# Raw weights in one ring of four halves, in a hybrid decoder step on one core of Trainium2

## The chip, the core and the metric

The kernel runs on one NeuronCore of one Trainium2 chip. The time is the device time of one execution in microseconds (us), from the first to the last instruction with what the launch adds around it. The engines of the core are named as in the profile: PE (TensorE, matrix products; PEld are its weight loads), ACT (ScalarE), DVE (VectorE), POOL (GpSimd) and SP (SyncE, which here only issues DMAs). The engines run their own instruction streams, each in its own fixed order, and wait for each other by semaphores.

## What is computed

One step of a decoder block over 520 tokens (512 of a new sequence, 8 single tokens that continue older ones), model width 1024, all in float32:

```python
h = x
h = h + 0.5 * swiglu(rms_norm(h, ffn1_norm), w_gate1, w_up1, w_down1)   # FFN width 2816
h = h + mixer(rms_norm(h, mix_norm), ...)     # causal pooling heads beside SSD (Mamba-2) heads
h = h + 0.5 * swiglu(rms_norm(h, ffn2_norm), w_gate2, w_up2, w_down2)
y = rms_norm(h, final_norm)

def swiglu(x, wg, wu, wd):
    return (silu(x @ wg) * (x @ wu)) @ wd
```

The change lies in how weights come on chip. Nearly all of its effect is to be looked for in the two FFNs and in the projections of the mixer.

## The kernel before

**Float32 by three products.** A weight block of 128 x 1024 arrives as raw float32 and is cut in two parts. ACT casts it to a rounded format (the tile `whi`), DVE subtracts the cast from the raw value and keeps the rest (`wlo`). A product then is three matmuls (`mm3`, lines 133, 136 and 137): high by high, high by low, low by high. Activations are cut in the same way.

**FFN tiles.** The 2816 columns are 22 tiles `f` of 128. A tile needs a gate block and an up block of 512 KB each: the pair that `raw_pair` returns, with the gate block in half 0 and the up block in half 1. Most tiles run through `Ffn.product`, which forms a block product of gate, up and x by seven products in place of eight (the scheme of Strassen and Winograd). Each product is 12 matmuls: products 1 and 2 use `d1` (the two parts of the gate block), 5 and 7 use `e1`, 6 and 3 use `e2` (parts of sums of the blocks, tiles `shi` and `slo`), 4 uses the second half of the up block (the quarter, tiles `qhi` and `qlo`).

The order on PE in the first FFN is written out in `stream`: product 1 of tile t, product 4 of the tile before, then 5, 6, 3, 7, 2 of tile t. Product 1 writes bank A; right after it ACT copies A, the snapshot of line 466, to the bank BE (or to the tile `ac`), and product 5 then accumulates on it. Product 7's snapshot must be taken before product 4 accumulates on bank A. Line 514 on DVE reads A when a tile is closed (`close`), and frees the bank for the tile after the next.

In the first FFN the tiles 0 and 1 run as plain float32 products (`plain`), tiles 2 to 21 through `stream`. After tiles 8 and 16 come four Down tiles each, `Down(c, d)`, which put the first 16 columns of blocks through the down projection in the same seven-product scheme (in the profile: `Down(c=0, d=0)` and so on). The last part of the down projection, and all of it in the second FFN, goes by units of one block (`load_unit`, line 129).

**What a tile does with its raw pair** (`load`, `sums`, `quarter`), for the first FFN from tile 4 on:

- SP issues two DMAs at line 367, half 0 and then half 1.
- ACT casts half 0 to `whi` (line 373) and writes its negative to `wlo` (line 374); a DMA that POOL issues adds the raw block to it in flight from HBM (line 375, an accumulating DMA). For a plain tile only the second 512 columns of `wlo` go this way, and DVE subtracts the first 512 (line 377); for a Down tile all 1024 go through ACT and the DMA (`n2` is 0).
- DVE forms the sums s1 (line 403, from both halves), and s2 in two steps (lines 404 and 405, from s1 and half 0). ACT and DVE cut s1 and s2 in parts (lines 121 and 123).
- The second half of half 1 is cut in `quarter`: ACT casts it (line 218 or 223) and DVE subtracts (line 224), or, for tiles up to 6, ACT and an accumulating DMA do it (lines 219 and 220).

So the last reader of half 0 is the second step of s2 at line 405, and that of half 1 is the quarter's low part at line 224 (for tiles up to 6 its cast).

**Raw buffers before.** `raw_pair` takes a new tile of two halves from the pool `wp`, with the tag `raw` and two buffers. A buffer is free for a new pair once every reader of both halves of the old pair is done. Units (`raw_tile`) take the halves of a pair one after the other, in the mixer too. The homes of `whi` and `wlo` are two buffers in the first FFN (`homes`, set ahead of `ffn1`), so tile t + 2 casts into the home of tile t once PE has run product 2 of tile t.

**The order of each engine.** The program is written as one stream. The framework (`TileContext(nc, schedule_with_timeline_sim=True)`) then lays down each engine's order ahead of time: a model of the timeline lets each engine take, among the instructions that are ready, the one of highest priority, which is by default the one written first. SP's DMAs are ordered in this way too. `tc.issue_after(i)`, inside `queued(...)`, puts the instructions of its block behind `i` on the engine of `i`. `tc.high_priority()` and `tc.keep_in_program_order()` do what they say. On the chip the order is fixed: an instruction whose data are late holds all that stand behind it on its engine.

**The second FFN** runs tile 0 as a plain product, woven into the end of the mixer (`LAST_PLAN`), and tiles 1 to 21 through `step`. The pair of tile 0 (`2_0`) is read by PE itself until the end of that weave.

Of the kernel before, what the change touches and what calls it, by code (L numbers as in the profile page):

```python
# [10 lines left out]
F32 = mybir.dt.float32  # L11
# [6 lines left out]
P = 128  # L18
# [45 lines left out]
def tile_trunk_step(ctx: ExitStack, tc: tile.TileContext, ins: dict, outs: dict):  # L64
    nc = tc.nc
# [6 lines left out]
    wp = ctx.enter_context(tc.tile_pool(name="wp", bufs=3, side="right"))  # L72
# [19 lines left out]
    def queued(*ins):  # L92
        stack = ExitStack()
        for i in ins:
            stack.enter_context(tc.issue_after(i))
        return stack

    def raw_pair(name):
        return wp.tile([P, 2, 1024], F32, tag="raw", bufs=2, name=f"raw_{name}")

    half, ends, added = [], [], []

    def raw_tile(name):
        if not half:
            t = raw_pair(name)
            half.extend([t[:, 1], t[:, 0]])
        return half.pop()
# [3 lines left out]
    def weight_homes(n, name, hp, nb, tags):  # L111
        if hp is wp:
            hp, nb, tags = homes.pop(0) if len(homes) > 1 else homes[0]
        return tuple(hp.tile([P, 1024], F32R, tag=t, bufs=nb, name=f"{t}_{name}")[:, :n] for t in tags)

    def split(src, n, name, hp, nb, tags, then=()):
        hi, lo = weight_homes(n, name, hp, nb, tags)
        h, l = hi, lo
        if len(src.shape) == 3:
            h, l = (t.rearrange("p (j c) -> p j c", j=src.shape[1]) for t in (hi, lo))  # L120
        cast = nc.scalar.copy(h, src)  # L121
        with queued(*then):
            low = nc.vector.tensor_tensor(out=l, in0=src, in1=h.bitcast(F32), op=ALU.subtract)
        ends[:] = cast.ins, low.ins
        return hi, lo
# [6 lines left out]
    def mm3(ps, whi, wlo, xhi, xlo, start, stop, pin=False, **kw):  # L132
        first = nc.tensor.matmul(ps, whi, xhi, start=start, stop=False, **kw)  # L133
        if pin:
            tc.keep_in_program_order(first)
        nc.tensor.matmul(ps, whi, xlo, start=False, stop=False, **kw)  # L136
        nc.tensor.matmul(ps, wlo, xhi, start=False, stop=stop, **kw)  # L137

    def ws(w, k, m=P):
        return w[:, k * m : (k + 1) * m]  # L140
# [102 lines left out]
    class Ffn:  # L243
# [15 lines left out]
        def plain_load(self, f, j=None, us=(0, 1), queue=nc.sync):  # L259
            if f not in self.raw:  # L260
                self.raw[f] = raw_pair(f"{self.i}_{f}")
            src = ins[f"w{self.i}gu"]
            for u in us:
                if j is None:
                    nc.sync.dma_start(out=self.raw[f][:, u], in_=src[2 * f + u])
                    continue
                q = (t.rearrange("p (q c) -> p q c", q=2)[:, :, j * P : j * P + P]
                     for t in (self.raw[f][:, u], src[2 * f + u]))
                queue.dma_start(out=next(q), in_=next(q))
# [86 lines left out]
        def load(self, f, first, then, by_dma):  # L356
            i, wx, src = self.i, self.wx, ins[f"w{self.i}gu"]
            n = f"{i}_{f}"
            raw = raw_pair(n)
            if isinstance(f, int):  # L360
                drams = [src[2 * f + u] for u in range(2)]
            else:
                lo = f.c * CHUNKS[0]
                drams = [ins[f"w{i}d"][2 * f.d + u, :, lo * P : (lo + 8) * P] for u in range(2)]
            self.dram[f] = drams
            for u in range(2):
                nc.sync.dma_start(out=raw[:, u], in_=drams[u])
            with queued(*first):
                if self.folded and (f, 0) not in LOW_ON_DVE:
                    d1 = weight_homes(1024, f"{n}a", wp, 3, ("whi", "wlo"))  # L370
                    hi, lo = d1
                    n2 = 512 if isinstance(f, int) else 0
                    nc.scalar.copy(hi, raw[:, 0])
                    nc.scalar.activation(out=lo[:, n2:], in_=hi[:, n2:].bitcast(F32), func=AF.Copy, scale=-1.0)
                    nc.gpsimd.dma_start(out=lo[:, n2:], in_=drams[0][:, n2:], accum_op=ALU.add)
                    if n2:
                        nc.vector.tensor_tensor(out=lo[:, :n2], in0=raw[:, 0, :n2], in1=hi[:, :n2].bitcast(F32), op=ALU.subtract)
                else:
                    d1 = split(raw[:, 0], 1024, f"{n}a", wp, 3, ("whi", "wlo"))
            with queued(*then, *(ends if by_dma and i == 1 else ())):  # L380
                self.sums(f, n, src, raw, d1, by_dma)
# [56 lines left out]
        def product(self, f, p):  # L438
            js = range(KD // 2)
            if f not in self.A:  # L440
                self.load(f, *self.behind.get(f, ((), (), False)))
                n = f"{self.i}_{f}"
                self.A[f] = ps[0].tile([P, 512], F32, tag="A", bufs=2, name=f"A{n}")
                self.BE[f] = ps[0].tile([P, 2, 512], F32, tag="BE", bufs=2, name=f"BE{n}")
                self.ac[f] = [self.wx.tile([P, 2, HB], F32, tag="ac", bufs=3, name=f"ac{n}_{q}") for q in range(2)]
            if p != 1 and 4 not in self.w[f]:
                self.quarter(f, self.held[f])
            slot, dst, opens = {1: (0, 0, True), 2: (1, 1, True), 5: (3, 2, True), 6: (5, 0, False),
                                3: (2, 2, False), 7: (4, 0, False), 4: (6, 0, False)}[p]
            opens = opens and (p != 2 or self.i == 2 or f in self.whole)  # L450
            out = self.A[f] if dst == 0 else self.BE[f][:, dst - 1]
            (whi, wlo), k = self.w[f][p]
            xth, xtl = self.nx[:2]
            for j in js:
                if isinstance(f, int):
                    x = xth[:, j, slot], xtl[:, j, slot]
                else:
                    x = (self.gs[f.c * CHUNKS[0] // 2 + j][:, q, {5: 6, 6: 5}.get(slot, slot)] for q in range(2))
                mm3(out[:, :HB], ws(whi, k[j]), ws(wlo, k[j]), *x, opens and j == 0,
                    j == KD // 2 - 1, pin=j == 0 and ((f, p) in ((2, 7), (3, 1)) or self.i == 1), skip_group_check=True)  # L460
            a, c = self.ac[f]
            if p == 1 and self.i == 1 and f not in self.whole:
                a = self.BE[f][:, :, :HB]
            keep = {1: a[:, 0], 6: a[:, 1], 7: c[:, 0], 5: c[:, 1]}.get(p)
            if keep is not None:
                self.copied = nc.scalar.copy(keep, out[:, :HB]).ins  # L466
            if p == 7:
                nc.vector.tensor_tensor(out=c[:, 0], in0=c[:, 0], in1=c[:, 1], op=ALU.add)

# [950 lines left out]
```

## Time and profile before

| | us |
|---|---|
| median of 3 runs | 978.33 |
| lowest and highest of them | 976.18 and 979.62 |
| the profiled execution | 978.69 |
| its span, first to last instruction | 976.9 |

The span and what lies around it (978.69 - 976.9 = 1.8 us) make up the time of the profiled execution. All times in the profile count from the start of the span. A row of the timeline gives start, duration, engine, line, operation and tiles (written <- read), and in brackets the idle time of the engine ahead of it with what ended it. A row of the waits gives who waited for whom: us in total, times, the longest. `PE A L137` is the instruction of PE at line 137 that writes tile A. A row of the stretches gives the stretch, its length, then for PE, PEld, DVE, ACT and POOL the busy us with the number of instructions, then the granted clock of PE, the share of the DMA engines and GB/s. A matmul of 260 columns has a duration of 0.28 us in the records, but matmuls overlap: where PE does not wait, they start 0.12 us apart, so waits of PE are read from the starts and from the number of matmuls in a stretch, not from its busy time alone.

### The profile page before, as it was taken

The numbers are of one execution on the slowest core, as the hardware profiler recorded it, in microseconds if no ns is written. First come the engines' busy times: TensorE is split into PE (matmuls) and PEld (weight loads), VectorE is DVE, ScalarE is ACT, GpSimd is POOL, SyncE is SP. The second block draws the span as 40 slices with busy tenths as digits, with TensorE's granted clock in tenths as the row PEclk, the third lists the DMA queues.
The fourth block names the chain that finished last, engine by engine and source line by source line (L and its number), as shares of the span: only waits on it lengthen the run. The fifth ranks groups of instructions, "written<-read, shape, count | busy, mean of one in ns | idle before, by whom it ended". The sixth has DMA issues, their size and how long they took to land.

```text
span 976.9 us, 19565 instructions
## 1 busy us (share of the span) xinstructions
PE 962.3 (99%) x7772; PEld 942.0 (96%) x7772; DVE 825.3 (84%) x1372; ACT 592.2 (61%) x1098; POOL 113.5 (12%) x192
## 2 busy tenths in 40 slices
PE   9999999999999999999999999999999999999996
PEld 8999999999999999999999999999999999999995
DVE  6899879998798688789978897999957999667886
ACT  7777656677566455485767565666643666515563
POOL 0111100001000000065331000100012000110010
PEclk9999999999999999999999999999999999999998
DMA  7565554445553343262443333433445433452232
GB/s 211 164 164 135 146 152 124 129 142 135 136 151 99 100 130 120 91 210 78 138 138 133 108 104 108 148 104 113 130 134 189 132 109 108 125 183 81 81 118 89
DMA packets 48444, 126.80 MB, mean 130 GB/s; under 512 B 7064, under 2 KB 15192, under 8 KB 48352
## 3 DMA queue, kind: packets, MB, share of 16 engines
q1 hardware_dynamic: 39840, 104.18, 31.7%
q0 software_dynamic: 8240, 21.24, 10.9%
q8 instruction: 61, 1.00, 0.4%
q14 instruction: 31, 0.25, 0.1%
q10 hardware_dynamic: 272, 0.13, 0.0%
HBM read 118.18 MB, written 7.34 MB: 128 GB/s over the span
## 4 chain that ended last, share of the span: by engine, by line
PE 68%; DVE 3%; DMA 1%; issue 1%; ACT 0%; DVEq 0%; SPq 0%; ACTq 0%
PE A L137 5%; PE A L133 5%; PE A L136 5%; PE dn L137 4%; PE dn L133 4%; PE dn L136 4%; PE BE L137 4%; PE BE L136 4%; PE BE L133 4%; PE wo L133 2%; PE wo L137 2%; PE wo L136 2%; PE inx L133 2%; PE inz L133 2%; PE inz L136 2%; PE inz L137 2%
## 5 line engine op out<-in xcount | busy, mean ns | idle before, releaser
L137 PE MATMUL dn<-g,wlo_2d 128*128 128x260 f32 x256 | 72.4, 283 | 0.0
L133 PE MATMUL dn<-g,whi_2d 128*128 128x260 f32 x256 | 72.1, 282 | 0.0
L136 PE MATMUL dn<-g,whi_2d 128*128 128x260 f32 x256 | 72.1, 282 | 0.0
L466 ACT COPY ac<-A 128x260 f32<-128x260 f32 x104 | 38.5, 372 | 31.1 <-PE A L137 29.4
L403 DVE TENSOR_TENSOR s<-raw 128x1024 f32<-128x1024 f32 x39 | 47.6, 1220 | 7.9 <-DMA raw<-in_w1gu 5.8
L133 PEld LDWEIGHTS dn<-g,whi_2d 128*128 128x128 f32 x256 | 48.2, 188 | 0.0
L136 PEld LDWEIGHTS dn<-g,whi_2d 128*128 128x128 f32 x256 | 48.2, 188 | 0.0
L137 PEld LDWEIGHTS dn<-g,wlo_2d 128*128 128x128 f32 x256 | 48.1, 188 | 0.0
L609 DVE SCALAR_TENSOR_TENSOR td<-dn,r_f 128x520 f32<-128x520 f32 (+1 forms) x25 | 16.8, 677 | 32.7 <-PE dn L137 32.7
L121 ACT CAST whi_2d<-raw_2d 128x1024 fp32r<-128x1024 f32 (+1 forms) x18 | 18.5, 1026 | 36.7 <-PE dn L136 15.0
L1148 POOL DMA_DIRECT2D out_nss<-hs x16 | 8.7, 545 | 259.3 <-DVE hs L1146 259.2
L133 PE MATMUL wo<-catg,whi_wo 128*128 128x260 f32 x128 | 37.1, 290 | 0.0
L133 PE MATMUL inz<-xh_mx,whi_inz 128*128 128x260 f32 x128 | 36.6, 286 | 0.0
L133 PE MATMUL inx<-xh_mx,whi_inx 128*128 128x260 f32 x128 | 36.4, 284 | 0.0
L137 PE MATMUL wo<-catg,wlo_wo 128*128 128x260 f32 x128 | 36.3, 283 | 0.0
L136 PE MATMUL inz<-xl_mx,whi_inz 128*128 128x260 f32 x128 | 36.2, 283 | 0.0
L137 PE MATMUL inz<-xh_mx,wlo_inz 128*128 128x260 f32 x128 | 36.2, 283 | 0.0
L136 PE MATMUL inx<-xl_mx,whi_inx 128*128 128x260 f32 x128 | 36.1, 282 | 0.0
L137 PE MATMUL inx<-xh_mx,wlo_inx 128*128 128x260 f32 x128 | 36.1, 282 | 0.0
L136 PE MATMUL wo<-catg,whi_wo 128*128 128x260 f32 x128 | 36.1, 282 | 0.0
L466 ACT COPY ac<-BE 128x260 f32<-128x260 f32 x41 | 15.4, 375 | 26.9 <-PE BE L137 18.5
L995 DVE SCALAR_TENSOR_TENSOR A<-U,h,A 128x544 f32<-128x544 f32 x36 | 28.9, 802 | 2.2 <-ACT A L993 1.8
(2154 smaller groups left out, 4377.8 us busy)
## 6 DMA issues: line engine op xcount, KB each, us to landing
raw<-in_w2gu SPq DMA_DIRECT2D x44, 512.0 KB, 4.4
raw<-in_w1gu SPq DMA_DIRECT2D x41, 512.0 KB, 4.5
raw_2d<-in_w2d SPq DMA_DIRECT2D x16, 512.0 KB, 4.5
raw_wo<-in_w_out SPq DMA_DIRECT2D x12, 512.0 KB, 4.3
ab<-scr_acs SPq DMA_DIRECT2D x8, 512.0 KB, 3.6
h<-in_state_ssm SPq DMA_DIRECT2D x16, 256.0 KB, 3.2
raw_inz<-in_w_in SPq DMA_DIRECT2D x8, 512.0 KB, 4.5
hs<-in_state_ssm POOLq DMA_DIRECT2D x16, 256.0 KB, 3.6
```

The source lines that it names most:

```text
L121: cast = nc.scalar.copy(h, src)
L133: first = nc.tensor.matmul(ps, whi, xhi, start=start, stop=False, **kw)
L136: nc.tensor.matmul(ps, whi, xlo, start=False, stop=False, **kw)
L137: nc.tensor.matmul(ps, wlo, xhi, start=False, stop=stop, **kw)
L403: nc.vector.tensor_tensor(out=s1, in0=diag, in1=up0, op=ALU.add)
L466: self.copied = nc.scalar.copy(keep, out[:, :HB]).ins
L609: nc.vector.scalar_tensor_tensor(out=o, in0=s, scalar=-0.5, in1=q, op0=ALU.mult, op1=ALU.mult)
L995: nc.vector.scalar_tensor_tensor(out=A[:, :n], in0=U[:, j : j + n], scalar=w(j), in1=A[:, :n], op0=ALU.mult, op1=ALU.add)
L1148: tc.keep_in_program_order(nc.gpsimd.dma_start(out=outs["nss"][:, b, 4 * g : 4 * g + 4], in_=hs))
```

## The change

All raw weights get one tile for the whole kernel, of two pairs of two halves, in place of a new tile per pair from two buffers. `raw_pair` counts its calls and returns the two pairs in turn; the framework then follows readers and writers by the part of the tile that they touch, so the DMA of a half waits for the readers of that half alone. One name, `2_2` (tile 2 of the second FFN), does not count: it gets the pair of the call before it, that of tile 1.

Two more edits come with it. In the first FFN the cast of tile 4's gate block, with the negated copy and the accumulating DMA that depend on it, is put behind the snapshot of product 7 of tile 2 on ACT. And for Down tiles with d = 3 (two of the eight), `n2` becomes 512: the first 512 columns of the low part are subtracted on DVE (line 377), and ACT's negated copy and the accumulating DMA carry only the other 512.

```diff
+    raws = wp.tile([P, 2, 2, 1024], F32, tag="raw", bufs=1, name="raw")
+    turns = []
+
     def raw_pair(name):
-        return wp.tile([P, 2, 1024], F32, tag="raw", bufs=2, name=f"raw_{name}")
+        if name != "2_2":
+            turns.append(name)
+        return raws[:, len(turns) % 2]
...
                 if self.folded and (f, 0) not in LOW_ON_DVE:
                     d1 = weight_homes(1024, f"{n}a", wp, 3, ("whi", "wlo"))
                     hi, lo = d1
-                    n2 = 512 if isinstance(f, int) else 0
-                    nc.scalar.copy(hi, raw[:, 0])
+                    n2 = 512 if isinstance(f, int) or f.d == 3 else 0
+                    with queued(*((self.tail,) if f == 4 else ())):
+                        nc.scalar.copy(hi, raw[:, 0])
...
             if keep is not None:
                 self.copied = nc.scalar.copy(keep, out[:, :HB]).ins
+                if (f, p) == (2, 7):
+                    self.tail = self.copied
```

## The prediction

> **What bounds the kernel now.** I read the page first, for the span and the engines:
>
> ```profile
> span 976.9 us, 19565 instructions
> PE 962.3 (99%) x7772; PEld 942.0 (96%) x7772; DVE 825.3 (84%) x1372; ACT 592.2 (61%) x1098; POOL 113.5 (12%) x192
> ```
>
> TensorE (PE) sets the time: it is busy in 962.3 of 976.9 us, and every other engine has room on the average. So a change can win only what PE waits, and can lose anything that makes it wait more. Where it waits I took from the table by stretches; its number in brackets after PE busy counts the matmuls.
>
> ```profile
> 54.00:114.00 60.00, 59.90 (x497) 59.52 (x496) 56.34 (x89) 45.61 (x74) 7.56 (x9) 1.00 0.57 141
> 114.00:167.00 53.00, 51.90 (x425) 51.06 (x424) 45.69 (x72) 30.73 (x49) 4.19 (x5) 1.00 0.54 148
> 167.00:229.00 62.00, 61.78 (x510) 61.18 (x509) 58.23 (x92) 43.63 (x72) 5.03 (x6) 1.00 0.49 134
> 229.00:292.00 63.00, 61.44 (x508) 60.83 (x507) 52.49 (x82) 37.81 (x60) 5.04 (x6) 1.00 0.53 139
> 292.00:355.00 63.00, 63.00 (x528) 63.00 (x528) 48.90 (x93) 34.35 (x65) 2.10 (x3) 1.00 0.34 102
> 653.00:714.00 61.00, 61.00 (x510) 61.00 (x509) 55.16 (x77) 39.44 (x67) 0.00 (x0) 1.00 0.32 104
> ```
>
> The clock column is 1.00 throughout. In the last two stretches PE never waits and does 528/63.00 = 8.38 and 510/61.00 = 8.36 matmuls per us, one per 0.12 us. At 8.37 the second stretch should hold 444 matmuls and has 425, a loss of 19 x 0.12 = 2.2 us; the fourth should hold 527 and has 508, also 2.2 us; the first lacks 5 (0.6 us), the third 9 (1.1 us). All four lie in the first FFN's streamed tiles. The second FFN (last row) loses nothing. What ends those waits is in the view of waits of the weight loads:
>
> ```profile
> PEld BE L133 <- ACT BE L466: 2.2, 4, 0.9
> PEld BE_Down(c=1, d=2)_2976 L133 <- ACT BE_Down(c=1, d=2)_2976 L466: 1.2, 1, 1.2
> PEld A L133 <- ACT ac L466: 0.9, 2, 0.7
> PEld A L133 <- DVE gq L514: 0.8, 3, 0.3
> PEld BE L137 <- DVE slo_2c L123: 0.5, 1, 0.5
> PEld BE_Down(c=0, d=2)_1441 L133 <- ACT BE_Down(c=0, d=2)_1441 L466: 0.4, 1, 0.4
> PEld A L137 <- DMA qlo_6b<-in_w1gu: 0.3, 1, 0.3
> ```
>
> Four of the seven rows name ScalarE's (ACT) snapshot at line 466, which copies the finished product 1 out of bank A so that product 5 may accumulate on it: 2.2 + 1.2 + 0.4 = 3.8 us in six tiles, and one more of 0.7 us at the start. Why the snapshot is late, the timeline of ACT and PE at one of the six shows:
>
> ```profile
> 272.10 1.05 ACT L373 CAST whi_18a<-raw 128x1024 fp32r<-128x1024 f32 x1 [1.50 <-DMA raw<-in_w1gu]
> 273.18 0.64 ACT L374 ACTIVATE wlo_18a<-whi_18a 128x512 fp32r<-128x512 f32 x1
> 273.72 0.37 ACT L466 COPY BE<-A 128x260 f32<-128x260 f32 x1
> 270.51 0.28 PE L137 MATMUL BE_Down(c=1, d=3)_3100<-gs,wlo_Down(c=1, d=3)a 128*128 128x260 f32 x1
> 273.38 0.28 PE L137 MATMUL A_Down(c=1, d=3)_3099<-gs,qlo_Down(c=1, d=3)b 128*128 128x260 f32 x1
> 274.14 0.39 PE L133 MATMUL BE<-xth_f,shi_17c 128*128 128x260 f32 x1 [0.48 <-ACT BE L466]
> ```
>
> ACT idles 1.50 us for the raw weights of the next tile, 18, then casts them, makes their negated copy, and only then takes tile 17's snapshot, which stands behind them in its order. PE, due at 273.50, starts at 274.14: 0.64 us late, and its first matmul takes 0.39 instead of 0.28 us. The cast could have run from 270.79, when PE ended its last use of the weight home that the cast overwrites (270.51 + 0.28). A tile whose weights had landed in time shows that this order alone does no harm:
>
> ```profile
> 177.64 1.05 ACT L373 CAST whi_13a<-raw 128x1024 fp32r<-128x1024 f32 x1
> 178.73 0.63 ACT L374 ACTIVATE wlo_13a<-whi_13a 128x512 fp32r<-128x512 f32 x1
> 179.53 0.36 ACT L466 COPY BE<-A 128x260 f32<-128x260 f32 x1 [0.17 <-PE A L137]
> ```
>
> Here the snapshot waited for PE, not PE for it. So in six tiles PE pays for a late load.
>
> **The change part by part.** *The ring.* Before, a pair of halves (gate weights, up weights) is one buffer, and both halves load when the last reader of the pair is done. Tile 17's pair, which frees tile 19's:
>
> ```profile
> 267.63 0.68 DVE L224 TENSOR_TENSOR qlo_Down(c=1, d=3)b<-raw_Down(c=1, d=3)_3074,qhi_Down(c=1, d=3)b 128x512 fp32r<-128x512 f32 x1
> 268.23 0.69 DVE L405 TENSOR_TENSOR s<-s,raw 128x512 f32<-128x512 f32 x1
> 277.27 0.68 DVE L224 TENSOR_TENSOR qlo_17b<-raw,qhi_17b 128x512 fp32r<-128x512 f32 x1
> 282.54 1.05 ACT L373 CAST whi_19a<-raw 128x1024 fp32r<-128x1024 f32 x1 [1.14 <-DMA raw<-in_w1gu]
> 283.84 1.22 DVE L403 TENSOR_TENSOR s<-raw 128x1024 f32<-128x1024 f32 x1 [0.76 <-DMA raw<-in_w1gu]
> ```
>
> The gate half's last reader is the sum at line 405, done at 268.92; the up half's is the quarter's low part at line 224, done at 277.95. So the gate half of tile 19 may load 277.95 - 268.92 = 9.0 us sooner, and the cast that came 1.0 to 1.5 us late finds its data. On SP's queue the gate half stands behind the up half of the tile before, which waits for the qlo of that pair (done 268.31, just ahead of 268.92), so the queue doesn't eat the gain. Per tile SP issues the same two DMAs. The up half then travels alone. What that is worth, from the DMA view (a gate half, to landing) and the chain (its up half, issued after it):
>
> ```profile
> raw<-in_w1gu SPq DMA_DIRECT2D x1, 512.0 KB, 3.7
> 268.34 0.33 SPq L367
> 268.71 4.37 DMA raw<-in_w1gu
> ```
>
> The second of a pair is issued 0.37 us later (268.34 to 268.71) and takes 4.37, so it lands 1.0 us after the first's 3.7; alone I cost it at 3.7 from the release, a gain of 1.0 us for the sum at line 403, which heads VectorE's (DVE) work on a tile. Its bounds are 0 (the gate half of the tile after, issued some 0.6 us later, slows it) and 1.0.
>
> The Trainium skill, page "DMA: Bandwidth & Descriptors", section "Bandwidth", speaks against parting a megabyte: batch to 1 MiB or more for three quarters of the peak. By the fit in its section "Anatomy of one DMA" (2.0 us plus bytes over 436 GB/s) a half alone is estimated at 3.2 us and a pair at 4.4, so the engines would lose 2.0 us a tile; the trace agrees in kind (1.0 us between the halves), and with a DMA share of 0.49 to 0.54 in these stretches it would not move the sum.
>
> *What it wins.* Six late snapshots: 3.8 us by the waits, plus 6 x 0.11 us for the slow first matmul, 4.4 us. The matmul counts say 2.2 + 2.2 = 4.4 for the two stretches that hold all six. I take 4.4.
>
> *The cast queued behind a snapshot.* The seventh wait, 0.7 us (0.8 with its slow matmul):
>
> ```profile
> 42.00 1.05 ACT L373 CAST whi_4a<-raw 128x1024 fp32r<-128x1024 f32 x1 [1.59 <-DMA raw<-in_w1gu]
> 42.95 1.05 ACT L121 CAST shi_3c<-s 128x1024 fp32r<-128x1024 f32 x1
> 44.43 0.35 ACT L466 COPY ac<-A 128x260 f32<-128x260 f32 x1
> ```
>
> whi_4a and shi_3c stand before tile 2's snapshot. The edit puts whi_4a, with its copy and accumulating DMA, behind it: 1.05 + 0.62 us sooner for the snapshot, more than the 0.7 that PE waited. Nothing is late for it: tile 4's weights are first used some 10 us on. Worth 0.8; at worst 0.
>
> *Half of a Down tile's low part (d = 3, two tiles) moves* from ACT and the accumulating DMA to DVE. ACT's copy falls from 1.06 to 0.64 us in the tile that had least room; DVE gains a subtraction of 128x512, as this row:
>
> ```profile
> 274.51 0.68 DVE L377 TENSOR_TENSOR wlo_18a<-raw,whi_18a 128x512 fp32r<-128x512 f32 x1
> ```
>
> 2 x 0.68 = 1.4 us of DVE time, hidden where DVE waits for a load (below), on the path where it doesn't.
>
> *What is late next.* DVE, in the Down tiles:
>
> ```profile
> 252.09 1.23 DVE L403 TENSOR_TENSOR s_Down(c=1, d=3)_3082<-raw_Down(c=1, d=3)_3074 128x1024 f32<-128x1024 f32 x1 [3.25 <-DMA raw_Down(c=1, d=3)_3074<-in_w1d]
> 263.66 1.22 DVE L123 TENSOR_TENSOR slo_Down(c=1, d=3)d<-s_Down(c=1, d=3)_3083,shi_Down(c=1, d=3)d 128x1024 fp32r<-128x1024 f32 x1
> 265.12 0.28 PE L137 MATMUL A_Down(c=1, d=3)_3099<-gs,slo_Down(c=1, d=3)d 128*128 128x260 f32 x1
> ```
>
> slo_Down(c=1, d=3)d ends at 264.88 and PE uses it at 265.12: 0.24 us to spare, and PE, no longer held 1.2 us in the tile before, would come 1.2 us sooner. DVE gets its 1.0 us per load, and the loads follow one another, so most of this is covered; I charge 0.25 us in each chunk, 0.5 in all. Bounds: 0, and 2.4 (all that the two chunks' last stalls gave).
>
> *Elsewhere.* The waits on gq (0.8 us), qlo_6b (0.3) and slo_2c (0.5) have other causes; I leave them, and their end for the range is 1.6 us. In the mixer and the second FFN units load half by half and sooner, but PE waits for none of them (510 matmuls in 61.00 us), so this is worth 0. Tile 2 of the second FFN, the exception in the diff, shares the halves of tile 1; its load waited for tile 1's last low part before, too:
>
> ```profile
> SPq L367 <- DVE wlo_1b L123: 13.6, 1, 13.6
> ```
>
> **Sum**, on the profiled execution, 978.69 us (span 976.9 and 1.8 around it): -4.4 - 0.8 + 0.5 = -4.7, that is 974.0. The median of the runs shown, 978.33, is 0.4 lower, within their spread of 976.18 to 979.62; from it the sum gives 973.6. I predict 974.0.
>
> **Rivals.** *(1) DVE takes the place of ACT.* If the up half gains nothing, DVE's chain (load, sum, quarter, next load) keeps its pace in the Down tiles and PE waits for slo where it waited for the snapshot. For it: the 0.24 us above. Against it: DVE idles 3.25 us for that load. Then 2.4 us of the gain go: 976.4.
>
> *(2) The casts wait in the wrong place: slower.* With data always there, the order of ACT, laid down ahead of time, decides. Between the freed weight home and product 5 lie two products of 12 matmuls, 24 x 0.12 = 2.9 us; cast, copy and snapshot need 1.05 + 0.64 + 0.37 = 2.1, in a Down tile with the full copy 2.5. If one more cast of 1.05 us (an shi) is put between, PE waits 0.2 us in each of 20 tiles (18 plain ones and the two Down tiles with the short copy) and 0.6 in each of the other 6 Down tiles, 7.6 us, less the 0.8 won at the start: 985.5. It decides once what is put between exceeds 0.8 us (0.4 in a Down tile). Against it: tiles like 13 already run in this order without a wait.
>
> *(3) It doesn't do what it says.* If SP's order keeps both halves behind the quarter's low part, the casts stay late and only the 0.8 at the start is won: 977.9.
>
> **How the numbers follow.** Forecast 0.62 (972.4 to 975.4: the sum with 1.6 us more, to the bound below); rival 1 0.18; rival 3 0.08; rival 2 0.12. A measurement of this kernel tells about 0.3% from no change, 2.9 us: below 975.4 is faster, above 981.3 slower. Faster: 0.62 and 0.04 of rival 1, 0.66. Slower: rival 2, 0.12. Same: 0.22. The range leaves out rival 2 and a thin tail: 971.5 to 979.0.
>
> **What would show it.** Right: the four snapshot rows are gone from the waits; stretches 114 to 167 and 229 to 292 hold some 18 more matmuls each; casts at line 373 start without an idle time ended by a raw DMA; gate halves are issued some 9 us ahead of their up halves. Wrong: PE waits on slo at line 123 (rival 1), the snapshot rows spread over many tiles (rival 2), or both halves still issued together (rival 3). A new wait in the mixer or the second FFN, which I cost at nothing, would also break it.

## The result and the profile after

| | before | after |
|---|---|---|
| median | 976.72 (8 runs, 976.15 to 979.62) | 974.47 (8 runs, 973.66 to 975.49) |
| profiled execution | 978.69 | 974.41 |
| its span | 976.9 | 972.6 |

The ratio is 0.9973, 95% interval 0.9962 to 0.9984: 2.6 us won, just short of the 0.3% (2.9 us) named in the prediction, while the interval excludes no change. A second comparison of the same pair gave 0.9972 (0.9960 to 0.9983). The two profiled executions lie 4.3 us apart, the medians 2.3. The predicted 974.0 is 0.5 below the measured median; the gain was predicted at 4.7.

The head of the page after: PE does the same 7772 matmuls, in 4.3 us less. Its idle time falls from 14.6 to 12.1 us and its busy time by 1.8, so the busy time alone doesn't show the waits here either.

```profile
span 972.6 us, 19624 instructions
PE 960.5 (99%) x7772; PEld 942.4 (97%) x7772; DVE 825.9 (85%) x1374; ACT 591.1 (61%) x1098; POOL 112.7 (12%) x192
```

The same stretches as in the prediction, after:

```profile
54.00:114.00 60.00, 60.00 (x500) 59.81 (x500) 56.62 (x91) 45.96 (x75) 7.56 (x9) 1.00 0.60 149
114.00:167.00 53.00, 52.91 (x441) 52.71 (x440) 48.93 (x77) 32.89 (x53) 4.19 (x5) 1.00 0.49 138
167.00:229.00 62.00, 61.78 (x510) 61.18 (x509) 57.70 (x91) 43.19 (x70) 5.03 (x6) 1.00 0.48 132
229.00:292.00 63.00, 63.00 (x528) 63.00 (x527) 55.78 (x86) 38.26 (x61) 5.88 (x7) 1.00 0.51 138
```

The second stretch went from 425 matmuls to 441, 3 short of the 444 of a PE that does not wait (a wait on gq is left in it), and the fourth from 508 to 528, which is that rate. The first gained 3; the third is as it was. These 36 matmuls of 0.12 us are 4.3 us, as much as the two spans differ: the gain lies in the two stretches that the prediction named, and what is won at the start and lost elsewhere about cancels. The waits of the weight loads that are left in the seven-product tiles of the FFNs, after:

```profile
PEld A L138 <- DVE gq L522: 0.8, 3, 0.3
PEld A L138 <- ACT ac L472: 0.4, 1, 0.4
PEld A L142 <- DVE slo_2d L128: 0.4, 1, 0.4
PEld A_Down(c=0, d=1)_1306 L138 <- DVE gq L522: 0.3, 1, 0.3
PEld BE L142 <- DVE slo_2c L128: 0.3, 1, 0.3
```

Every row of a snapshot in the first FFN's streamed tiles is gone. Of the five, the rows of gq stood before too. The three others all lie at the start of the second FFN (between 620 and 640 us), and two of them are not new: the waits of before between 600 and 645 us are

```profile
PEld BE L137 <- DVE slo_2c L123: 0.5, 1, 0.5
PEld A L133 <- ACT ac L466: 0.2, 1, 0.2
```

So this place cost 0.7 us before and costs 1.1 after.

Tile 18's cast, which came 1.50 us late before, in the timeline after:

```profile
266.98 1.05 ACT L379 CAST whi_18a<-raw 128x1024 fp32r<-128x1024 f32 x1
...
268.61 0.37 ACT L472 COPY BE<-A 128x260 f32<-128x260 f32 x1
269.78 0.28 PE L138 MATMUL BE<-xth_f,shi_17c 128*128 128x260 f32 x1
262.18 0.93 SPq L372 DMA_DIRECT2D raw<-in_w1gu  x2
272.87 0.93 SPq L372 DMA_DIRECT2D raw<-in_w1gu  x2
```

The cast carries no bracket, so it waited for no load, and no cast at line 379 in the streamed tiles has idle time ended by a raw DMA (ten had at line 373 before); the snapshot is done at 268.98, 0.8 us before PE wants it, and PE's first matmul takes 0.28 us instead of 0.39. The last two rows show the ring on SP's queue. Each row is two issues, an up half of one tile and, 0.6 us behind it, the gate half of the tile after: gate half 19 goes out at 262.8, its up half at 272.9, 10 us later (9.0 were predicted).

### The profile page after: what moved, and what is told of

It is laid out like the page before. It is cut to its first block, busy times and chain, and to the rows that moved or that the text cites. A ratio compares the mean times of both kernels' runs of the same rounds, so it can differ in the third digit from the quotient of the medians.

```text
span 972.6 us, 19624 instructions
## 1 busy us (share of the span) xinstructions
PE 960.5 (99%) x7772; PEld 942.4 (97%) x7772; DVE 825.9 (85%) x1374; ACT 591.1 (61%) x1098; POOL 112.7 (12%) x192
## 4 chain that ended last, share of the span: by engine, by line
PE 95%; DVE 3%; ACT 1%; DMA 0%; issue 0%; POOL 0%; DVEq 0%; ACTq 0%
PE A L142 8%; PE A L138 8%; PE A L141 8%; PE BE L141 6%; PE BE L142 6%; PE BE L138 6%; PE dn L142 4%; PE dn L138 4%; PE dn L141 4%; PE P L288 4%; PE wo L138 2%; PE wo L142 2%; PE wo L141 2%; PE inx L138 2%; PE inz L138 2%; PE inz L141 2%
## 5 line engine op out<-in xcount | busy, mean ns | idle before, releaser
L126 ACT CAST whi_2d<-raw 128x1024 fp32r<-128x1024 f32 (+1 forms) x18 | 18.5, 1026 | 37.6 <-PE dn L141 15.0
```

## The experiments

All ratios are to the kernel before. Three groups each shared a chip and the runs of before on it: the first four kernels (before's median there is 978.56), the next four (977.79) and the last two (977.08).

| kernel | median | ratio (95%) |
|---|---|---|
| before again | 977.32 | 0.9996 (0.9985 to 1.0007) |
| ring alone | 978.31 | 0.9998 (0.9987 to 1.0008) |
| both edits without the ring | 978.98 | 1.0005 (0.9997 to 1.0014) |
| after, gate half behind the up half | 997.58 | 1.0192 (1.0174 to 1.0210) |
| after again | 975.43 | 0.9972 (0.9960 to 0.9983) |
| after without the Down edit | 975.04 | 0.9967 (0.9955 to 0.9980) |
| before, casts behind snapshots | 1009.03 | 1.0301 (1.0276 to 1.0326) |
| after, close first | 977.42 | 0.9994 (0.9981 to 1.0006) |
| after without the exception | 975.70 | 0.9985 (0.9976 to 0.9994) |
| before, queued cast alone | 979.92 | 1.0028 (1.0017 to 1.0040) |

**Before, profiled three more times.** The question was why 4.7 us of waits were worth 2.6. The kernel is before, unchanged.

> The kernel before, unchanged, profiled a second time. Forecast was 4.7 us and the profiled executions differ by 4.3, but the medians only by 2.25. Theory: the late snapshots of the kernel before hang on when a load lands, which differs from execution to execution; the profiled one (978.69) was a late one. Then this profile, if its time is near the median of 976.7, shows the waits of the weight loads on the snapshot of line 466 at about 1.5 to 2.5 us in place of 3.8 in the tiles, and the rest of the span the same. Rival: the start of the kernel or its end differs between executions and the snapshot waits stay at 3.8 us. Time against before: 0 in either case.

This execution took 981.29 us (the kernel's median is 977.32), so it could not show one near the median. Its waits:

```profile
PEld BE L133 <- ACT BE L466: 1.9, 3, 1.1
PEld A L137 <- DMA qlo_5b<-in_w1gu: 1.7, 1, 1.7
PEld BE_Down(c=1, d=2)_2976 L133 <- ACT BE_Down(c=1, d=2)_2976 L466: 1.4, 1, 1.4
PEld dn L137 <- DVE wlo_2d L123: 1.3, 1, 1.3
PEld A L133 <- ACT ac L466: 1.0, 2, 0.8
PEld BE_Down(c=0, d=2)_1441 L133 <- ACT BE_Down(c=0, d=2)_1441 L466: 0.6, 1, 0.6
```

The tiles' snapshots sum to 1.9 + 1.4 + 0.6 = 3.9 again, so the idea that they had been long by chance in the first profile seemed to fall. Two long executions could not settle it, and two more were profiled.

> The kernel before once more, for a profile of an execution near its fastest (about 976). Two profiled executions of it took 978.69 and 981.29 us and both had the snapshot waits of the streamed tiles at 3.8 to 3.9 us; its medians are 976.7 to 978.6, so the measured gain of the change (2.3 to 2.6 us) is smaller than those waits. My theory: other waits than the snapshots make most of the spread (late accumulating DMAs as that of qlo_5b, 0 to 1.7 us, and a low part in the down projection, 0 to 1.3), and in an execution under 977 the snapshot waits themselves are shorter, 1.5 to 3 us, since they hang on when a load lands. Rival: the snapshot waits are 3.8 us in every execution, and the fast ones gain elsewhere.

978.32 us, not an execution near the fastest. The tiles' snapshots now cost 0.9 + 0.8 + 0.2 (one more row of a Down tile) = 1.9:

```profile
PEld A L137 <- DMA qlo_5b<-in_w1gu: 1.6, 1, 1.6
PEld A L133 <- ACT ac L466: 1.0, 2, 0.8
PEld BE_Down(c=1, d=2)_2976 L133 <- ACT BE_Down(c=1, d=2)_2976 L466: 0.9, 1, 0.9
...
PEld BE L133 <- ACT BE L466: 0.8, 2, 0.6
```

> The same once more, for the same question: the snapshot waits of the streamed tiles beside the time of the execution. My theory: they go with the time (1.5 to 3 us under 977, near 3.9 above 978). Rival: 3.8 us whatever the time.

975.20 us, span 973.4, only 0.8 above the profile after. The tiles' snapshots cost 0.6 + 0.4 = 1.0, and there is no late accumulating DMA:

```profile
PEld A L133 <- ACT ac L466: 1.1, 2, 0.9
...
PEld BE L133 <- ACT BE L466: 0.6, 2, 0.4
...
PEld BE_Down(c=1, d=2)_2976 L133 <- ACT BE_Down(c=1, d=2)_2976 L466: 0.4, 1, 0.4
```

Why the same kernel waits or doesn't, tile 11 shows. First the timeline of the execution that the prediction was made from:

```profile
158.15 1.05 ACT L373 CAST whi_11a<-raw 128x1024 fp32r<-128x1024 f32 x1 [1.76 <-DMA raw<-in_w1gu]
160.19 0.39 PE L133 MATMUL BE<-xth_f,shi_10c 128*128 128x260 f32 x1 [0.73 <-ACT BE L466]
```

and its DMA view around the issue of that gate half:

```profile
raw<-in_w1gu SPq DMA_DIRECT2D x1, 512.0 KB, 5.7
```

Then the same two instructions in the fourth profile:

```profile
155.49 1.05 ACT L373 CAST whi_11a<-raw 128x1024 fp32r<-128x1024 f32 x1
158.28 0.28 PE L133 MATMUL BE<-xth_f,shi_10c 128*128 128x260 f32 x1
```

The gate half took 5.7 us to land in the one; in the other the pair's two halves have a median of 3.8. With the shorter load the cast is in time and PE doesn't wait. The load ahead of another of the six snapshots, that of Down(1, 3) for the snapshot of Down(1, 2), goes the same way: 5.1 us and a wait of 1.2 in the first profile, 4.1 us and a wait of 0.4 in the fourth. So the waits that the change removes depend on how long a load takes, and that scatters from execution to execution. What makes a load longer no run shows. The four profiled executions of before, put together:

| time | snapshots, tiles and the rows of `ac` | other late data | what is left |
|---|---|---|---|
| 975.20 | 1.0 + 1.1 | 0 | 973.1 |
| 978.32 | 1.9 + 1.0 | 1.6 (qlo_5b) | 973.8 |
| 978.69 | 3.8 + 0.9 | 0.3 (qlo_6b) | 973.7 |
| 981.29 | 3.9 + 1.0 | 1.7 (qlo_5b) + 1.3 (wlo_2d) | 973.4 |

Of each row of `ac`, 0.2 us lie in the second FFN and the rest at the start. Without these waits every one of the four comes to 973.1 to 973.8. (The plain tiles' waits for raw data, 0.4, none, 0.9 and 0.5 us in the order of the table, are left in; without them too it would be 972.7 to 973.8.) That is nearly all of the spread of these four, and it would explain why after's runs scatter so little (1.8 us between the extremes, before 3.5 on the same chip): the ring issues the gate half 10 us sooner, so that 2 us more for a load do no harm. The expectation for the fourth profile held in direction at most: its value (1.0) is below the range given for it, and the third, at 978.32, has 1.9 where near 3.9 was expected above 978.

**The ring alone.** The cast isn't queued, and the Down tiles keep their low part:

```diff
-                    n2 = 512 if isinstance(f, int) or f.d == 3 else 0
-                    with queued(*((self.tail,) if f == 4 else ())):
-                        nc.scalar.copy(hi, raw[:, 0])
+                    n2 = 512 if isinstance(f, int) else 0
+                    nc.scalar.copy(hi, raw[:, 0])
```

> The ring of four halves alone; the cast of tile 4 is not queued and the Down tiles with d = 3 keep the full negated copy. Theory: the early gate half does the work, so the six snapshot waits are gone here too and the time is within 0.8 us of the changed kernel's (974.5 to 975.3); at most the wait at 43.8 us in the start is left. Rival: the two other edits are needed, because the full copy of 1.06 us in a Down tile leaves 0.4 us of room or because tile 4's cast now comes even earlier: then 975.5 or more.

It gains nothing, as the rival had it. The late snapshots of the tiles are gone as in after (441 and 527 matmuls in the two stretches), but one row has grown:

```profile
PEld A L138 <- ACT ac L471: 3.3, 2, 2.8
```

and the timeline of ACT says how:

```profile
42.68 1.04 ACT L378 CAST whi_4a<-raw 128x1024 fp32r<-128x1024 f32 x1 [3.74 <-DMA raw<-in_w1gu]
43.63 0.37 ACT L471 COPY ac<-A 128x260 f32<-128x260 f32 x1
```

The planner now puts tile 4's cast ahead of one more snapshot of tile 2; that it does so because a half that is free sooner looks early to its model is inferred from the order. On the chip the data aren't there yet; ACT idles 3.74 us and the snapshot stands behind it. With the queued cast the order is turned round, in the timeline of after:

```profile
40.50 0.38 ACT L472 COPY ac<-A 128x260 f32<-128x260 f32 x1 [1.07 <-PE A L142]
...
44.50 1.05 ACT L379 CAST whi_4a<-raw 128x1024 fp32r<-128x1024 f32 x1
```

On the ring the queued cast is worth 0.9998 against 0.9967 (the ring with it and without the Down edit, below; each against its own group's before), 3.0 us. The traces put both halves of the story in place. The 400th matmul of PE (in tile 5) starts at 65.02 us before, at 67.34 with the ring alone and at 64.45 with the ring and the queued cast; the 2400th (in tile 20) at 311.45, 309.03 and 306.53. So in the tiles between them the ring alone wins 4.7 us over this execution of before, and what it loses, 2.3 us, it loses at the start.

**The queued cast alone, on before's buffers:**

```diff
-                    nc.scalar.copy(hi, raw[:, 0])
+                    with queued(*((self.tail,) if f == 4 else ())):
+                        nc.scalar.copy(hi, raw[:, 0])
...
+                if (f, p) == (2, 7):
+                    self.tail = self.copied
```

> The kernel before with one edit alone: the cast of tile 4's gate half queued behind tile 2's snapshot of product 7. The prediction's term for it was 0.8 us won, at worst 0. My theory after the ring alone and the two edits without the ring: on the kernel before the queued cast takes away the snapshot wait of 0.7 to 0.8 us at the start, but moves shi_3c and shi_3d on ACT and tile 4's first DVE work, and tile 3's product 6 then waits for slo_3d (1.1 us without the ring but with both edits), so that it wins nothing: ratio 0.999 to 1.002, the row of slo_3d there. Rival: the term holds, ratio 0.9985 to 0.9995 and no row of slo_3d; then the loss of the two edits without the ring came from the Down tiles' edit.

It loses 2.7 us. The snapshot at the start is in time, but all that depends on the cast is later, and PE waits for that:

```profile
PEld A L137 <- DMA qlo_6b<-in_w1gu: 1.5, 1, 1.5
PEld A L137 <- DVE slo_3d L123: 1.1, 1, 1.1
```

The row of slo_3d is the one expected; the loss is a little above the range given. Two smaller rows, qlo_4b (0.6) and slo_6d (0.5), are in none of the four profiles of before. A late accumulating DMA such as qlo_6b's belongs to the scatter above, in part; how much of it is the edit's, these profiles can't tell.

**Both edits without the ring:**

```diff
-    raws = wp.tile([P, 2, 2, 1024], F32, tag="raw", bufs=1, name="raw")
...
-        return raws[:, len(turns) % 2]
+        return wp.tile([P, 2, 1024], F32, tag="raw", bufs=2, name=f"raw_{name}")
```

> The two other edits on the buffers of before, without the ring. Theory: the wait of 0.7 us (0.8 with its slow matmul) at the start goes, and the two Down tiles with d = 3 wait 0.4 us less each; the other late snapshots stay: 0.8 to 1.6 us under the kernel before, and rows of the wait on the snapshot in four tiles. Rival: these edits carry the gain, and the ring little: then within 0.5 us of the changed kernel.

Nothing won: the start's wait on the snapshot of tile 2 is gone, but slo_3d costs 1.1 here too. Nor do the Down tiles with d = 3 wait less: their snapshots have rows of 0.7 and 0.5 us, where the first profile of before has none. A miss of mine, and of a piece with the cast alone. So neither the ring nor the cast wins anything by itself, and together they win 2.6 us.

**The Down edit left out of after:**

```diff
-                    n2 = 512 if isinstance(f, int) or f.d == 3 else 0
+                    n2 = 512 if isinstance(f, int) else 0
```

> The ring and the queued cast, without the edit of the Down tiles (the full negated copy of 1.06 us in all eight). The ring alone had no snapshot wait in the Down tiles, but one of 2.8 us at tile 2, where the cast of tile 4 stood ahead of a snapshot and waited for its data. Theory: the queued cast takes that wait, and the Down edit is worth nothing by itself: within 0.5 us of the changed kernel, no wait on a snapshot in the tiles. Rival: the Down edit carries 0.5 to 1.5 us, seen as waits on the snapshot or on slo in tiles 9 and 17.

975.04 against 975.43 for after beside it: the edit is worth nothing, as expected. Of the kernels that ran, this is the smallest with the gain. After itself, measured again beside it, was expected as follows.

> The changed kernel, unchanged, beside the same runs of the kernel before as the three below. The two profiles of the kernel before show the same 3.8 and 3.9 us of snapshot waits in the tiles and differ elsewhere (qlo_5b 1.7, wlo_2d 1.3 in the second only), so its spread of 976 to 981 lies in other waits. Theory: the gain from the snapshots is there in every execution, so the ratio is 0.9955 to 0.9975 here too. Rival: the gain of the first measurement was luck of the runs, then 0.9985 or more.

0.9972, inside the range. But the snapshots' waits are not the same in every execution of before, as the third and fourth profiles showed later.

**The gate half queued behind the up half**, the ring's early gate half undone:

```diff
-            for u in range(2):
-                nc.sync.dma_start(out=raw[:, u], in_=drams[u])
+            up = nc.sync.dma_start(out=raw[:, 1], in_=drams[1])
+            with queued(up.ins):
+                nc.sync.dma_start(out=raw[:, 0], in_=drams[0])
```

> The changed kernel with one thing taken back: SP issues a tile's up half first and the gate half behind it, so the gate half waits for the quarter's low part again, and lands a little later than before the change (by the 1.0 us between two halves). Theory (an early gate half is what removes the waits): the snapshot waits come back in the six tiles, each up to 1 us longer than before, so 2 to 6 us over the kernel before, 979 to 983. Rival (the gain comes from the up half alone travelling alone, or from the other edits): the waits stay away and the time stays within 1 us of the changed kernel's, 974 to 975.5.

The direction is as expected, the size far above it. The snapshot waits come back in nine tiles and more:

```profile
PEld BE L138 <- ACT BE L473: 6.4, 9, 1.6
PEld A_Down(c=0, d=0)_1182 L142 <- DMA wlo_Down(c=0, d=0)a<-in_w1d: 3.7, 1, 3.7
PEld A L138 <- ACT ac L473: 3.0, 3, 2.1
```

So without the early gate half the snapshots are late again: it is what holds the gain. Why the loss is so much larger than the gain is not shown; the engines' orders are laid down anew and differ from before's, PE waits for an accumulating DMA too, and its clock falls for a while (last section).

**Before, with each gate cast behind the snapshot of the tile before.** If only ACT's order mattered, this would win without a ring:

```diff
-                    nc.scalar.copy(hi, raw[:, 0])
+                    with queued(*((self.opened,) if f != 4 else (self.tail,))):
+                        nc.scalar.copy(hi, raw[:, 0])
...
+                if p == 1:
+                    self.opened = self.copied
```

> The kernel before with its two buffers and its late loads, in which each gate cast of the first FFN stands behind the snapshot of the tile before it on ScalarE (that of tile 4 behind the snapshot of product 7 of tile 2). Theory (a late load costs only because the cast stands ahead of a snapshot): the waits on the snapshot go although every load is as late as before, 3 to 5 us under the kernel before. Rival (the late load costs by itself, through VectorE's sums): waits on slo or qlo take their place, and less than 1.5 us is won.

It falls badly. No tile's snapshot is late any more, but a cast that comes later also makes the negated copy later and the DMA that POOL then issues, and PE needs that `wlo` in product 1. All eight Down tiles wait for it, 20.4 us in all, a wait that neither the theory nor the rival named; the two longest:

```profile
PEld A_Down(c=0, d=0)_1191 L137 <- DMA wlo_Down(c=0, d=0)a<-in_w1d: 3.6, 1, 3.6
PEld A_Down(c=0, d=2)_1440 L137 <- DMA wlo_Down(c=0, d=2)a<-in_w1d: 3.5, 1, 3.5
```

So in the Down tiles neither order does without earlier data: cast before snapshot is late for PE by the snapshot, cast behind it by the accumulating DMA. The plain tiles are another matter. From tile 9 on none of them waits for its `wlo` here, one waits 0.6 us for another low part (slo_11d), and four of the six late snapshots of before lay in them. A kernel with this order in those tiles alone was not run, so that the ring is needed for their part of the gain is not shown.

**After without the exception for 2_2:**

```diff
-        if name != "2_2":
-            turns.append(name)
+        turns.append(name)
```

> The changed kernel with every call counted, so that tile 2 of the second FFN (2_2) takes the pair of halves after that of tile 1, which is the pair of tile 0. In the changed kernel's profile the load of 2_2 is issued at 601.8 us, after tile 1's low part, and the pair of tile 0 is read by PE until 619.7. My theory: the exception is what keeps the start of the second FFN covered. Without it the load of 2_2 is issued 18 us later, at about 620, lands at 623.5, and its low part on DVE is done at about 626, where PE wants it at 623.1: 2 to 3 us lost in the stretch 615 to 635, and 976.5 to 978.0 in all (ratio to the kernel before 0.999 to 1.001). Rival: the planner, which knows of the late load, gives PE other work of tiles 0 and 1 meanwhile, and the exception is worth nothing: 974.5 to 975.5 (ratio 0.997).

0.9985 lies between the two expectations, and its interval overlaps after's. The planner gives PE other work meanwhile (tile 2's product 1 starts at 627.0 us against 618.4), and what is left in place at the start of the second FFN is

```profile
PEld BE L137 <- ACT ac L471: 1.1, 2, 0.6
PEld BE L140 <- DVE xtl_f L228: 0.7, 1, 0.7
```

1.8 us against 1.1 in after. Nearer the rival: the exception is worth about 0.7 there; what the rest of the 1.2 us is stays open, since the orders of PE, ACT and DVE differ elsewhere too.

**An attempt at a better kernel**, the cut of `slo` put behind the close in four tiles, against the waits on gq that are left:

```diff
-                e1 = split(s1, 1024, f"{n}c", wx, 2, ("shi", "slo"))
+                e1 = split(s1, 1024, f"{n}c", wx, 2, ("shi", "slo"), (self.shut,) if i == 1 and f in ((0, 1), 12, 14, 16) else ())
...
-            nc.vector.tensor_tensor(out=tg[:, 0], in0=self.A[f][:, :HB], in1=tg[:, 0], op=ALU.mult)
+            self.shut = nc.vector.tensor_tensor(out=tg[:, 0], in0=self.A[f][:, :HB], in1=tg[:, 0], op=ALU.mult).ins
```

> The changed kernel, with one more order: in four tiles (Down(0, 1), 12, 14 and 16) the low part slo of the first sum stands behind the close of the tile two before it on VectorE, whose product with bank A frees the bank that PE waits for. The changed kernel waits 0.8 + 0.3 us there, and each wait has a slow matmul of 0.1 behind it. Theory: those waits go and 1.1 to 1.6 us are won over the changed kernel. Rival: slo then comes late by its own duration of 1.22 us and PE waits for it: no gain, or a loss up to 1 us.

It loses after's gain: 977.42 against 975.43, more than the rival allowed. Three waits of 0.3 became one of 2.1, at tile 14, where the planner laid DVE's order anew:

```profile
PEld A L138 <- DVE gq L522: 2.1, 1, 2.1
```

No kernel that was tried beats the change by more than its interval.

## Why the prediction came out as it did

**The bound and its place: right.** Of the four rows of snapshots the three of the tiles are gone, and so are the 0.7 us at the start of the fourth. The two stretches hold 16 and 20 more matmuls (18 were named), casts start without a wait for a load, gate halves go out 10 us ahead.

**"Six late snapshots: 4.4": right in mechanism and for the execution that it was read from, too large against the median.** Between the two profiles the first FFN wins what the sum says: PE's 2400th matmul starts at 306.62 us in place of 311.45, 4.8 us sooner, where 4.4 + 0.8 - 0.5 = 4.7 was predicted. (The matmul counts that were held against the 4.4 have a wait on gq of 0.3 in them, which stayed.) But the waits in that execution, 3.8 us, were one draw: they are 3.8, 3.9, 1.9 and 1.0 in four executions, 2.7 in the mean. That 978.69 lay near the median of the three runs shown hid that it was a long one; more runs put the medians at 976.7 to 978.6. After's profile is at its median (974.41 and 974.47), before's is 2.0 above its own (978.69 and 976.72), and this 2.0 is the distance between the 4.3 us of the two profiles and the 2.3 of the medians. How long the loads took in that one execution was in the sum, unmarked.

That the predicted time lies 0.5 us from the median is in part luck. The sum takes the waits on snapshots out of one execution (3.8 + 0.9 us, which leaves 974.0). Taken out of the other three they leave 973.1, 975.4 and 976.4, since two of these also wait 1.6 or 1.7 us for qlo_5b, and one 1.3 us for wlo_2d, of which the sum has nothing.

**"The cast queued behind a snapshot: 0.8, at worst 0": wrong as a term of its own.** Alone it costs 2.7 us; on the ring it saves about 3. "Nothing is late for it" is the step that fails alone: slo_3d is, by 1.1 us. And I priced it against before's order of ACT, which the ring changes: the planner moves the cast ahead of one more snapshot that PE needs.

**"DVE, 0.5 charged": not seen.** No row of slo is left in the first FFN after, so rival 1 did not happen; nor did rivals 2 and 3. DVE has the data sooner too: from 54 to 355 us its sums idle 1.4 to 2.9 us for loads in the three profiles with the gain, 10.4 to 13.3 us in the four of before.

**The Down edit, without a gain in the sum: right**, by the kernel without it.

**"Elsewhere, 0": wrong, 0.4 to 1.5 us lost.** How much sooner than in the first profile of before, in us:

| profile | PE's 2400th matmul | PE's last matmul | the end of the span |
|---|---|---|---|
| after | 4.8 | 5.2 | 4.3 |
| after again | 5.3 | 4.8 | 3.8 |
| after without the Down edit | 4.9 | 5.3 | 4.6 |

The start of the second FFN takes 0.4 us (1.1 against 0.7), which the mixer gives back in two of the three (in after again it loses 0.4 more). The steady loss lies behind PE. PE's last matmuls in the fourth profile of before,

```profile
963.96 0.71 PE L842 MATMUL psl<-sq_last,ones 128*128 128x260 f32 x2 [0.62 <-ACT sq_last L826]
```

and after:

```profile
962.25 0.71 PE L850 MATMUL psl<-sq_last,ones 128*128 128x260 f32 x2 [0.62 <-ACT sq_last L834]
```

PE ends 1.7 us sooner, the span (973.4 and 972.6) only 0.8. From PE's end to that of the span it is 8.8 us in all four profiles of before and 9.5 to 9.8 in the three of the table, where the last outputs are issued at other distances. But the queued cast alone has 9.6 with the outputs issued as before, so the cause stays open. On the other side the accumulating DMAs of tiles 5 and 6 are in time in all three profiles with the change and the queued cast. For tile 5's the DMA view of the third profile of before, and then of after, has:

```profile
qlo_5b<-in_w1gu POOLq DMA_DIRECT2D x1, 256.0 KB, 8.7
```

```profile
qlo_5b<-in_w1gu POOLq DMA_DIRECT2D x1, 256.0 KB, 5.8
```

Before, it is issued 0.6 us behind a pair of halves and shares the DMA engines with both; after, only with the up half, since the gate half of that tile went out earlier. I had left that wait (qlo_6b, 0.3) alone as having "other causes".

**The rule against parting a megabyte** (the Trainium skill, page "DMA: Bandwidth & Descriptors", section "Bandwidth") did not decide. The DMA share for halves that travel apart is higher in the first of the four stretches (0.60 against 0.57) and lower in the other three, and no cast in the streamed tiles waits for a load. The fit that the prediction took from the same page is given there for DMAs that GpSimd issues; SP issues these halves, and one alone (at 608.7 us in after) took 3.5 us, where 3.2 was estimated.

## What to carry to other kernels

A wait for a load that one profiled execution shows is one draw: take a second and third execution, or the spread of the times, before its microseconds go into a sum, and count steadier times as part of what an earlier load brings. Where a planner lays down the order, check the order again after the data come earlier: here one cast moved ahead of a snapshot that PE needed, and cost what the ring had won. An order mended without earlier data can move the wait to the next reader, as it did in the Down tiles. Before a reader is put behind another instruction, follow everything that it feeds, above all a DMA that it triggers.

## What the runs showed of the hardware

After some long waits PE runs at half its clock for a while. In the kernel with the gate half queued behind the up half, PE waits 3.7 us in Down tile (0, 0), until 113.5 us; stretches of 1 us around it:

```profile
113.00:114.00 1.00, 0.51 (x3) 0.51 (x4) 0.18 (x1) 0.00 (x0) 0.00 (x0) 0.82 0.00 0
114.00:115.00 1.00, 1.00 (x6) 1.00 (x6) 0.00 (x0) 0.00 (x0) 0.00 (x0) 0.50 0.00 0
...
118.00:119.00 1.00, 1.00 (x11) 1.00 (x10) 0.69 (x2) 0.47 (x1) 0.84 (x1) 1.00 0.00 0
```

From about 113.6 to 117 the granted clock is 0.50. (In so short a stretch the number in brackets misleads, since it counts every matmul that touches the stretch.) By their starts 13 matmuls begin between 114 and 117 us, where 25 would at 0.12 us each: 12 x 0.12 = 1.4 us are lost on top of the wait of 3.7. The Trainium skill, page "TensorE: Matmul & The Clock Gate", section "What's actually happening", states this: half rate after an idle window of about 3.4 us, full rate after a busy one. The trace agrees in the length of the slow time. It doesn't in the wait that brings it on: in the kernel with the casts behind the snapshots, PE waits 2.6 us in Down tile (1, 2) and the clock is 0.50 behind it, while the wait of 3.6 us in Down tile (0, 0) leaves it at 1.00:

```profile
271.00:272.00 1.00, 0.86 (x4) 0.86 (x5) 1.00 (x4) 0.00 (x0) 0.00 (x0) 0.50 0.00 0
...
112.00:113.00 1.00, 0.81 (x6) 0.81 (x7) 1.00 (x2) 0.00 (x0) 0.00 (x0) 1.00 0.00 0
```

So here the length of a wait alone doesn't say whether the clock falls. It adds to the cost of the two kernels with many long waits, and the mean clock is lowest in one of them: 0.984 to 0.993 in the five runs with the casts behind the snapshots, against 0.996 or 0.997 in every run of after. With the prediction's waits, of 1.2 us at most, the clock is 1.00 in every stretch that it shows.
